# Laying out split operands so that the addresses of a matmul's moving operand and of the next weights keep one difference

## The chip, the core and the metric

The kernel runs on one core of a Trainium2 chip. The core has five engines with their own instruction streams: TensorE (PE in the profile; PEld is its weight load), VectorE (DVE), ScalarE (ACT), GpSimd (POOL) and SyncE (SP), which here only issues DMAs. They share the on-chip memory SBUF (128 partitions; an operand is a stretch of bytes in each partition) and wait for each other through semaphores. TensorE multiplies a stationary operand, the weights (128x128, loaded by a weight load of its own that runs while the previous matmul streams), with a moving operand (128 x up to 512) and adds into PSUM. The metric is device time in microseconds; lower is better.

## What is computed

One layer of a decoder trunk in float32: D = 1024, 512 positions and 16 meta tokens ahead of them. All products below have to be good to float32 accuracy.

```python
h = concatenate([meta, x])                   # (1, 528, 1024)
u = rms_norm(h, norm_gain)
rq, rk, rv, rg, gq, gk, gv, gg, glr, m_ret, m_gla = split(u @ w_in)
o_ret = retention(rope(rq), rope(rk) / 16, rv)         # 4 heads, 256 keys, 512 values
o_ret = head_group_norm(o_ret) * silu(rg)
log_a = log_sigmoid(glr @ w_gate_up + b_gate) / 16
o_gla = gla(gq, gk, gv, log_a)                         # 4 heads, 128 keys, 256 values
o_gla = head_rms_norm(o_gla) * silu(gg)
merged = sigmoid(m_ret) * (o_ret @ w_branch_ret) + sigmoid(m_gla) * (o_gla @ w_branch_gla)
out = rms_norm(h + merged @ w_out)[:, 16:]
```

Nearly all the arithmetic is in the projections `u @ w_in` (11,280 columns), the two branch products and `w_out`.

## The kernel before

**Split operands.** TensorE works on float32 operands in a rounded form (`float32r`). To keep accuracy each operand x is split into `hi`, its rounded form (a copy on ACT), and `lo = x - hi` (a subtraction on DVE): `split`, L154. A product then takes three passes, hi·hi, hi·lo and lo·hi, into one PSUM sum. `mm3` (L189, L192, L193) issues them in that order; `quad` (L318), `proj_a` (L425) and the first projection (L640) write them out.

**`quad`.** Most projections go through `quad`, which forms two 256-column blocks of the result from 7 products instead of 8 (Strassen's scheme in Winograd's form). The activations stand in seven split forms: A11, A12, A22 and the sums S1 to S4. Each product takes one form and one 512x256 block of weights or a sum of blocks (made on DVE), splits that block with `prepare`, and then does 2 column tiles x 4 k x 3 passes = 24 matmuls. With `rows` the activation form is the stationary operand and the weights' block moves (256 columns); otherwise the block's columns are stationary and the form moves (256 columns, or 264 where `wide` takes the meta tokens along). Order of the products: A11, A12, S2, S3, S1, A22, S4; with `early` A11, S3, S2, A12, S1, A22, S4.

**Where operands lie.** Split weights come from `wsplit`: one tile for hi and one for lo, tags `whi` and `wlo`, three buffers each, rows of 256 columns (1024 bytes). The normalized activations lie in `xh`, `xl` (two tiles each, of 4 k x 2 halves x 272 columns; a half is 1088 bytes, a k 2176), which hold A11, A12, A22 and A21; the sums S1 to S4 have tiles `fh3` to `fh6` and `fl3` to `fl6` (4 x 272). A21 is read by `proj_a` alone (`gq0`, `gk0`), not by any product of `quad`. The forms of the GLA branch lie in tiles that the GLA stage has freed (`form_tiles`), with rows of 1024 bytes. Retention heads 0 to 2 are turned into `oh`, `ol` (rows of 2048 bytes), head 3 into the places of `xh0` and `xl0`; the merged activations go to the places of `xh1`, `xl1` and two freed tiles, their sums to those of `fh3` to `fl6`.

**Order of the stages.** First projection and norms; `gla_qk(0)` with the forget gates woven in (`forget_gates`, whose ACT and DVE work is put in a written order by `act` and `vec`); GLA heads 0, 1 with `gla_g(0)`; `gla_qk(1)`, `gla_v(1)`; GLA heads 2, 3 woven into `gla_g(1)`, `gates_first` and `gla_branch` (which uses `quad` with the forms of the GLA output); then for each retention head `ret_qk`, `ret_g`, `ret_v` with the attention of the head before, and for heads 1 and 2 `gates_gla` in turn with `ret_branch` (128x512 matmuls with the turned head moving); `ret_branches` for heads 2 and 3; last the output projection: `wo_first` (256 columns by `mm3`), one `quad` (`wo1`), and the last 256 columns by `mm3`. `weave` alternates a dense generator (matmuls of projections) with a chain of attention steps.

In `forget_gates` the copies of S1 and S3 (`form`) are made ahead; S2 and S4 and the DVE parts of all four follow:

```python
        forms.append(form(S2, u00))
        next_weights(0)
        forms.append(form(S4, u01))
        for i in (2, 0, 1, 3):
            forms[i]()
```

## Time and profile before

| | us |
|---|---|
| median of 3 runs (763.56 to 764.13) | 763.91 |
| span of the profiled execution, first to last instruction | 762.2 |
| DVE busy | 611.2 |
| ACT busy | 451.2 |
| HBM read / written | 104.44 MB / 11.53 MB |

The profile holds one execution; its own time is given as the span, and what a run takes beside the span isn't in it. Times are microseconds from the span's start, means are in ns. A matmul's listed duration is longer than its share of PE, since matmuls overlap: the distance between starts is what counts. Two groups show the splits' price on both engines (columns: line, engine, operation, output<-inputs, shapes, count, then busy us and mean ns, then idle time of the engine ahead of them and who ended it):

```profile
L154 ACT CAST rv_h<-rv_w 128x1024 fp32r<-128x1024 f32 x24 | 25.2, 1052 | 26.9 <-DVE rv_w L371 9.6
L154 DVE TENSOR_TENSOR rv_l<-rv_w,rv_h 128x1024 fp32r<-128x1024 f32 x24 | 29.3, 1221 | 9.2 <-ACT rv_h L154 9.2
```

## The change

It moves operands to other addresses and reorders passes; the number and shapes of matmuls, splits and DMAs stay. In the new constants a lane is a step of `LANE` = 16 elements, 64 bytes, and counts modulo 4.

- `two_forms` puts hi and lo of a pair of forms into one tile, 2 x 2176 elements with 32 elements of gap, in alternating order; `s3` does so for S3 with rows of 288. So hi and lo of a form lie 2 lanes apart, as do neighbouring k.
- S4 has no tile of its own any more: it takes A21's place, and so is formed after `values(1)`, when `gk0` has read A21, and no longer beside S2.
- `wsplit` makes one tile `ws` of 2240 elements (three buffers) for hi and lo, shifted by a number of lanes that the caller gives: interleaved rows of 544 elements (hi at 0, lo at 288), or, with a second number `x`, hi and lo one behind the other at lanes of their own.
- `prepare` asks for the lane of the product's form + 3 with `rows`, + 1 otherwise; for the GLA branch and the output projection tables give the lanes (`G_AT`, `M_AT`).
- `quad` (without tables) and `proj_a` do the three passes of an odd k in the order lo·hi, hi·hi, hi·lo.
- Retention head 3, the merged activations and their sums share tiles that hold hi and lo together.

```diff
+BY_PRODUCT = {1: A11, 2: A12, 3: S4, 4: A22, 5: S1, 6: S2, 7: S3}
+X_AT = 3
+LANES = [X_AT + n for n in (0, 0, 1, 0, 1, 0, 1)]
+O_AT = 2
+M_AT = [(X_AT + 2, X_AT + 2), (1, 2)]
+G_AT = {A11: (1, 1), A12: (2, 2), S4: (2, 2), S1: (2, 2), S2: (2, 2), S3: (0, 2), A22: (0, 0)}
+PASSES = ((0, 0), (0, 1), (1, 0))
...
+    def two_forms(name, swap):
+        t = cp.tile([P, 2 * FW + 2 * LANE], F32R, tag=name, name=name)
+        return [t[:, o:o + FW].rearrange("p (k n c) -> p k n c", k=4, n=2)
+                for o in ((0, FW + 2 * LANE), (FW + 2 * LANE, 0))[swap]]
...
-    def wsplit(shape, name):
-        return (wp.tile(shape, F32R, tag="whi", name=f"{name}_h", bufs=3),
-                wp.tile(shape, F32R, tag="wlo", name=f"{name}_l", bufs=3))
+    def wsplit(shape, name, w=0, x=None):
+        t = wp.tile([P, WT], F32R, tag="ws", name=f"{name}_s", bufs=3)
+        o = LANE * ((w - W_AT) % 4)
+        if x is None:
+            v = t[:, o:o + 4 * 544].rearrange("p (k c) -> p k c", k=4)
+            return v[:, :, :256], v[:, :, 288:]
+        n = int(np.prod(shape[1:]))
+        parts = [t[:, a:a + n] for a in (o, o + n + LANE * ((x - w) % 4))]
+        return [a.rearrange("p (k c) -> p k c", k=shape[1]) if len(shape) > 2 else a for a in parts]
...
         def prepare(i, w):
-            hi, lo = wsplit([P, 4, 256], f"{name}_{i}")
+            form, d = BY_PRODUCT[i], 3 if rows else 1
+            at = (LANES[form] + d,) if lanes is None else [a + d for a in lanes[form]]
+            hi, lo = wsplit([P, 4, 256], f"{name}_{i}", *at)
...
-                    for j, (x1, x2) in enumerate(((0, 0), (0, 1), (1, 0))):
+                    passes = PASSES if lanes is not None or kk % 2 == 0 else PASSES[2:] + PASSES[:2]
+                    for j, (x1, x2) in enumerate(passes):
...
-    def branch(src, row0, oh, ol, name, evac, bank=ppt):
+    def branch(src, row0, oh, ol, name, evac, bank=ppt, at=0):
         for q in range(4):
             raw = wraw(f"{name}_{q}_w")
-            hi, lo = wsplit([P, 4, 256], f"{name}_{q}")
+            hi, lo = wsplit([P, 4, 256], f"{name}_{q}", at, at)
...
-        forms.append(form(S4, u01))
-        for i in (2, 0, 1, 3):
+        for i in (2, 0, 1):
             forms[i]()
...
         values(1)
+        form(S4, u01)()
...
-                    hi, lo = wsplit([P, 4, 256], f"br{h}_{q}")
+                    hi, lo = wsplit([P, 4, 256], f"br{h}_{q}", *((O_AT, O_AT), (X_AT, X_AT))[h - 2])
...
-        w = wsplit([P, 4, 256], f"wo{o}_{kh}")
+        w = wsplit([P, 4, 256], f"wo{o}_{kh}", *[a + 3 for a in M_AT[kh]])
```

## What I predict

> **What bounds the kernel now.** I read the page first (busy time, then the shares of the chain that ended last), then the chain of waits in order of time, then PE's timeline, because the change touches nothing but where matmul operands lie.

> ```profile
> span 762.2 us, 14057 instructions
> ...
> PE 750.4 (98%) x5595; PEld 701.5 (92%) x5595; DVE 611.2 (80%) x873; ACT 451.2 (59%) x764; POOL 133.4 (17%) x172
> ...
> PE 87%; DVE 9%; issue 2%; ACT 1%; POOL 0%; POOLq 0%; DVEq 0%
> ```

> PE is busy for 98% of the span and is 87% of the chain. DVE holds 9%. So the time is PE's number of matmuls times their start-to-start distance (I call it the pitch), and DVE is next behind. A matmul's own duration is no use here, since matmuls overlap; the chain's rows are, because a row is the time in which PE did 24 matmuls in a row (one "block": one product of `quad`, or one 24-matmul group elsewhere).

> ```profile
> 255.01 2.93 PE rqk_b L318 x24
> 257.94 2.92 PE rqk_c L318 x24
> ...
> 275.26 2.85 PE rg_b L318 x24
> ```

> ```profile
> 381.33 2.80 PE mg_c L318 x24
> ```

> A block of 128x256 matmuls takes 2.80 to 2.85 us (I take 2.83, 118 ns each); one with a moving operand 264 wide takes 2.92 (122 ns). Almost every block of the kernel looks like this, whatever the stage. A few don't:

> ```profile
> 232.76 5.70 PE bg_b L318 x48
> 238.46 2.82 PE bg_c L318 x24
> 241.28 2.74 PE bg_b L318 x24
> 244.02 2.72 PE bg_a L318 x24
> 246.74 2.72 PE bg_b L318 x24
> 249.46 2.83 PE bg_c L318 x24
> 252.29 2.73 PE bg_b L318 x24
> ```

> These are the second half of the GLA branch (`gla_branch`, j=1) at the same shape, the same clock and without waits, yet four blocks run at 2.72 to 2.74 (113.5 ns) and others at 2.83. What differs is addresses. Count an SBUF address in lanes: steps of 64 bytes, modulo 256 bytes, so lanes 0 to 3. For each matmul take the lane of the weights that are loaded meanwhile, those of the next matmul, less the lane of its own moving operand: D. In this branch every row of a tile is 1024 bytes and hi and lo are a multiple of 256 apart, so D is constant inside a block. Adding up the sizes of the tiles ahead in the pools gives D=1 for S2, A12, S1 and S4 (241.28, 244.02, 246.74, 252.29: all fast), D=3 for A22 (249.46) and D=2 for A11. The first block of the 5.70 row is S4 of j=0: also D=1, but slow (5.70 is twice 2.85). So D=1 held constant can run in two ways, 113.5 or about 118 ns, and it stays for the block in the one that it entered.

> Another constant stands in the output projection, where D=0:

> ```profile
> 734.74 0.28 PE L318 MATMUL wo_c<-wo_h,msh 128*128 128x256 f32 x1
> 734.86 0.28 PE L318 MATMUL wo_c<-wo_l,msh 128*128 128x256 f32 x1
> 734.98 0.28 PE L318 MATMUL wo_c<-wo_h,msl 128*128 128x256 f32 x1
> 735.10 0.28 PE L318 MATMUL wo_c<-wo_h,msh 128*128 128x256 f32 x1
> 735.22 0.28 PE L318 MATMUL wo_c<-wo_l,msh 128*128 128x256 f32 x1
> 735.34 0.28 PE L318 MATMUL wo_c<-wo_h,msl 128*128 128x256 f32 x1
> ```

> Starts 120 ns apart: D=0 is the slowest constant. Everywhere else D changes every three matmuls, because the activation tiles have rows of 1088 or 2176 bytes (17 or 34 lanes) and the weights rows of 1024 (16): the 118 of the other blocks is a mix.

> The 512-wide matmuls of the retention branches give the opposite preference. Head 2 (D=1) runs until 679.69, head 3 (D=0) after it:

> ```profile
> 676.89 0.39 PE L189 MATMUL br_p<-oh,br_h 128*128 128x512 f32 x1
> ...
> 679.69 0.39 PE L189 MATMUL br_p<-oh,br_h 128*128 128x512 f32 x1
> ...
> 681.07 0.39 PE L189 MATMUL br_p<-oh,br_h 128*128 128x512 f32 x1
> ...
> 683.79 0.39 PE L189 MATMUL br_p<-oh,br_h 128*128 128x512 f32 x1
> ```

> Twelve matmuls take 2.80 us with D=1 (233 ns) and 2.72 us with D=0 (227 ns).

> **The change, part by part.** It removes no matmul, split or transfer. It sets D.

> *256-wide blocks.* In the new layout hi and lo of an activation form lie 2 lanes apart, each row adds 2 lanes, and the weights' tile (`wsplit`) has the same steps: rows of 2176 bytes, lo 1152 bytes (2 lanes modulo 256) behind hi. With passes in the order hi-hi, hi-lo, lo-hi for even k and lo-hi, hi-hi, hi-lo for odd k, I walked through the six steps: each gives the same D, and the lane chosen in `prepare` (activation + 3 where the form is the stationary operand, + 1 where it moves) makes it 1. `G_AT` and `M_AT` do the same for the GLA branch and the output projection. There are 23 quads of 7 products, 161 blocks; 25 of them are 264 wide; with 4 of `gq0` and 8 of `wo_p` that leaves 148 blocks of 256. Six run at 2.72 or so already: three of j=1 besides the last, S4, and S2 and A12 of j=0. So 142 can gain, at most 2.83 - 2.72 = 0.11 us each, 15.6 us. Since D=1 has two rhythms I weigh them by what the trace has: of seven full-clock blocks with D=1, six are fast, but of four entries into such a stretch three ended fast. Between products D is off for one matmul wherever the forms' lanes differ (three times in a quad), so entries count too. I take 0.8 fast: a block of 2.74, gain 0.09, 142 x 0.09 = 12.8 us. Ends: all fast 15.6; none fast (2.83) 0.

> *264-wide blocks* (25, and 4 of `gk0`): no constant D of this width stands in the trace. The eight more columns cost 2.92 - 2.83 = 0.09 us a block now; the bounds are 2.72 + 0.09 = 2.81 and no change at 2.92. I take 0.8 of the way, 0.09 x 29 = 2.6 us (ends 0 and 3.2).

> *512-wide matmuls.* `branch` and `ret_branches` get D=0 for all heads: 96 matmuls each of heads 0, 1 and 2 go from 233 to 227, 288 x 6.6 ns = 1.9 us; head 3 has it already.

> Sum on PE: 12.8 + 2.6 + 1.9 = 17.3 us.

> [...]

> *What the sum loses.* Only 87% of the chain is PE. The rest is DVE, ACT and issue, mostly at the merge before the output projection, where the chain goes through DVE; a faster PE waits there. 17.3 x 0.87 = 15.1. Then there are stages in which DVE is full already (columns: PE, PEld, DVE, ACT, POOL busy):

> ```profile
> 40.00:60.00 20.00, 20.00 (x166) 19.87 (x166) 19.32 (x28) 18.47 (x30) 1.59 (x2) 1.00 0.54 109
> ...
> 280.00:300.00 20.00, 20.00 (x187) 18.94 (x186) 19.93 (x24) 13.25 (x20) 8.27 (x4) 1.00 0.39 107
> ...
> 600.00:620.00 20.00, 19.85 (x182) 18.52 (x181) 19.97 (x27) 13.49 (x24) 2.37 (x5) 1.00 0.40 123
> ```

> At 3% less PE time each would have to fit in some 19.4 us: over by 0.5 and 0.6 in the last two, near zero in the first. With the 19 us stages around 340, 460 and 720 I take 1.6 us. Left: 13.5 us.

> *The S4 form moves* from the middle of `gk0` to after `values(1)`, into the place of x's second half, first K half, which `gk0` has read by then. It issues no DMA, only two instructions:

> ```profile
> L682 ACT CAST fh<-u 128x1056 fp32r<-128x1056 f32 x4 | 4.3, 1073 | 0.0
> ```

> ```profile
> L685 DVE TENSOR_TENSOR fl<-u,fh x4: 1250/1250/1251, 40.1 to 43.6; 128x1056 fp32r<-128x1056 f32 x4
> ```

> ACT gets 1.07 us and DVE 1.25 us later. Behind them on DVE stand the adds and the split for `gg0`'s third product, behind them on ACT a table load and the first decays; if DVE gained nothing from the earlier gap, PE would be late by 1.25 us at that product. But DVE is the full engine of the 40 to 60 stage, so what was taken out ahead comes back: I take 0, ends -1.25 and +1.25. Its reader, the last product of `gg0`, comes some 20 us later.

> *Shared tiles.* hi and lo of split weights are now one tile of three buffers instead of two of three. If the first matmul of a block had to wait for lo as well, it would wait at most one matmul longer (118 ns; two where weights are stationary), as the next pass reads lo anyway. PE now waits for a lo in one place:

> ```profile
> PE bg_b L318 <- DVE bg_l L154: 1.3, 1, 1.3
> ```

> So: 0, end +1 us. The ACT and DVE operations keep their sizes; only row steps differ. After that wait PE also runs a stretch at half clock (granted 0.91 over that stage); whether it returns is worth up to 1.7 us either way:

> ```profile
> 220.00:240.00 20.00, 17.94 (x138) 17.54 (x137) 17.14 (x16) 10.69 (x14) 3.47 (x2) 0.91 0.84 203
> ```

> **Sum and time.** 13.5 us off the profiled span: 762.2 to 748.7. The median of the runs shown, 763.91, is 1.7 us above the span; I take the same there: **750.4 us**.

> **Rivals.**
> 1. *Fast everywhere, and the supply keeps up.* All blocks at 2.72: 15.6 + 3.2 + 1.9 = 20.7, between 18.0 (x 0.87) and 20.7 of it kept: 743.2 to 745.9. For it: once entered, the 113.5 ns rhythm never left by itself in the trace. Against it: S4 of j=0 at 2.85, and DVE's full stages.
> 2. *The 118 ns rhythm of D=1 is common.* A quarter to a half of the blocks fast: 142 x 0.0275 or 0.055, + 0.8 or 1.6, + 1.9 = 6.6 or 11.3; x 0.87 - 1.6 = 4.1 or 8.2: 755.7 to 759.8.
> 3. *Addresses don't matter*, or D is not what I worked out, and the fast blocks of the GLA branch have another cause (their tiles, their stage): 763.9. The heads' 2.80 against 2.72, in one stage, speaks against it. [...]
> 4. *Slower: constant D locks the streams in step in the worst place.* One mechanism, every block from `gv1` to the end: a constant D keeps whatever relation it enters, and the output projection shows one at 120 ns, above the mix. At 2.88 a block, 142 x 0.05 + 6 x 0.16 = 8.1, the 264s at 2.96 another 1.2, less 1.9 for the heads: +7.4 us, 771.3. It decides from a mean block of about 2.84 up. Against it: that is D=0, and no block with D=1 is that slow in the rows.

> **How the numbers follow.** Forecast (746 to 755.5) 0.56, rival 1 0.14, rival 2 (to 762) 0.14, rival 3 0.08, rival 4 0.08. About 0.2% is what a measurement of this kernel can tell from no change. Faster: 0.56 + 0.14 + 0.14 = 0.84; same 0.08; slower 0.08. Range: from rival 1's lower end, 743, to 760, rival 2's upper end; left out are rivals 3, 4 and edges, under 0.2.

> **What would show it.** Chain rows of 24: `rg`, `rv`, `mr`, `mg` at 2.72 to 2.75, `rqk` at 2.81 to 2.83, `wo` starts 113 to 114 ns apart instead of 120; branch matmuls of heads 0 to 2 at 227. DVE's share of the chain above 9%, with new PE waits for `rg_l` or `rv_l` near 290 and 605. I am wrong if blocks stay at 2.83 with D constant (rival 2 or 3), if they show 2.88 (4), or if PE gains but the span doesn't, with PE waiting on DVE (then the 0.87 is too high).

## The result, and the profile after

The changed kernel takes **766.35 us** (median of 6 runs, 766.18 to 766.46); the kernel before, beside it, 763.82 (763.20 to 764.13). The ratio is 1.0033, 95% interval 1.0021 to 1.0045: slower by 0.33%, where 1.8% faster was forecast. The page of the changed kernel, the lines that answer to those shown of before:

```profile
span 764.4 us, 14037 instructions
...
PE 751.2 (98%) x5595; PEld 702.2 (92%) x5595; DVE 611.7 (80%) x873; ACT 451.0 (59%) x764; POOL 133.8 (18%) x172
...
PE 82%; DVE 10%; ACT 4%; issue 3%; POOL 1%; POOLq 0%; DVEq 0%; ACTq 0%
```

The same number of matmuls, as much PE time as before, and less of the chain on PE (82% against 87%): PE got hardly faster, and a few waits were added. The chain in order of time shows both halves of this in the stage of `rqk` and `rg`:

```profile
259.60 2.94 PE rqk_c L347 x24
262.54 2.93 PE rqk_b L347 x24
...
277.00 2.82 PE rg_b L347 x24
279.83 2.82 PE rg_a L347 x24
282.65 2.82 PE rg_b L347 x24
285.47 2.82 PE rg_c L347 x24
```

The blocks that were to take 2.74 take 2.82, where before they took 2.83 and 2.85; the 264-wide ones take 2.93 to 2.94 as before. Yet the change does what it says: with the tiles' addresses put beside the matmuls of the trace, D is 1 at nearly every step inside these blocks. Their starts lie, over and over, 115, 123, 116, 118, 118 and 117 ns apart, 117.8 on average. Blocks near 113.3 are found only in the GLA branch and in the output projection, where the forms' rows are multiples of 256 bytes.

Three figures sum this up: the distances from each matmul's start to the next, summed by width (those above 1.3 times the median are waits and left out).

| us | before | after | mean before | mean after |
|---|---|---|---|---|
| 256 wide | 419.0 (3557 matmuls) | 417.8 (3551) | 117.80 ns | 117.66 ns |
| 264 wide | 84.3 (694) | 84.7 (694) | 121.5 ns | 122.1 ns |
| 512 wide | 154.0 (666) | 151.8 (662) | 231.2 ns | 229.3 ns |

The sums hold different numbers of matmuls, so the means are what to compare: the 256-wide matmuls gained 0.14 ns each, 0.5 us in all, and the 512-wide ones 1.9 ns each, 1.3 us.

And this is where the end moved by 2.2 us in the two profiled executions (start of the same matmul, after less before):

| stretch | us |
|---|---|
| start-up, to the first `gg0` product | +0.46 |
| `gg0`, products S2 and S3 (S4 form moved) | +0.79 |
| turning the GLA output (`got1`) | +0.39 |
| first branch blocks of heads 0 and 1 | +0.31, +0.38 |
| `rg3`, product A22 | +0.98 |
| branches of heads 2 and 3 | -0.54 |
| everything else | -0.55 |

The waits of PE name what is late: for `gg_s` and `rg_s`, splits on DVE, PE did not wait before.

```profile
PE bg_b L347 <- DVE bg_s L173: 1.3, 1, 1.3
...
PE rg_c L347 <- DVE rg_s L173: 0.8, 1, 0.8
...
PE gg_b L347 <- DVE gg_s L173: 0.4, 1, 0.4
```

## The experiments

Eleven kernels were run. Times are medians; each ratio is to the kernel before on the same chip.

**1. Lanes that stand still.** In the fast blocks of before not only D was constant: every row is 1024 bytes and hi and lo are a multiple of 256 apart, so both operands stay on one lane. In the change both hop by 2 lanes at most steps and only their difference stays. e1 lets them stand:

```diff
-FW = 8 * HW
+FW = 4 * 576
-        return [t[:, o:o + FW].rearrange("p (k n c) -> p k n c", k=4, n=2)
-                for o in ((0, FW + 2 * LANE), (FW + 2 * LANE, 0))[swap]]
+        return [t[:, o:o + FW].rearrange("p (k c) -> p k c", k=4)[:, :, :2 * HW]
+                .rearrange("p k (n c) -> p k n c", n=2) for o in (0, FW)]
-            at = (LANES[form] + d,) if lanes is None else [a + d for a in lanes[form]]
+            at = [LANES[form] + d] * 2 if lanes is None else [a + d for a in lanes[form]]
-                    passes = PASSES if lanes is not None or kk % 2 == 0 else PASSES[2:] + PASSES[:2]
+                    passes = PASSES
```

(S3's rows become 320 elements; the output projection's lanes follow.)

> Layout of the changed kernel, but with every row a multiple of 256 bytes and hi and lo in the same lane, so that not only D stays 1 inside a block but also the lane of the moving operand and the lane of the weights; passes in the old order. Theory A (the rhythm needs both lanes to stand still, and a constant D with both lanes jumping by two from matmul to matmul is no better than a mix): a good part of the 256-wide blocks falls from 2.83 to 2.72 us; half of 142 blocks would give -8 us, 758; three quarters 754. Theory B (D is all that counts, and the changed kernel sits in the 118 ns rhythm of D=1): blocks stay at 2.83, 765 to 767.

Measured: 761.71 us, ratio 0.9971 (0.9960 to 0.9982), 4.6 us under the change's median and faster than both kernels. Its chain in the stage shown above:

```profile
269.08 2.92 PE rqk_c L347 x24
272.00 2.74 PE rqk_b L347 x24
274.74 2.83 PE rg_b L347 x24
277.57 2.83 PE rg_a L347 x24
280.40 2.83 PE rg_b L347 x24
283.22 2.74 PE rg_c L347 x24
285.96 2.72 PE rg_b L347 x24
288.69 2.83 PE rg_c L347 x24
```

Now the two rhythms of the prediction appear, in every stage: of the stretches of 10 or more matmuls with D=1, 53 (1500 matmuls) run at 113.3 ns, 56 (1574) at 117.8, and 2 are mixed. So of these layouts D=1 gives the choice of 113.3 only with still lanes, and then about half the blocks take it. The mean distance of the 256-wide matmuls falls to 116.25 ns, 1.4 less than in the change, which is 5.0 us; the 8 us that the expectation put on half of the blocks did not all come.

**2. Constancy of D alone.** e4 is the change with the old order of passes; the lanes hop as before, and D repeats 1, 1, 3 (so every third step is off, not every sixth as the expectation has it):

```diff
-                    passes = PASSES if lanes is not None or kk % 2 == 0 else PASSES[2:] + PASSES[:2]
+                    passes = PASSES
```

> The changed kernel with the old order of passes for odd k, so that D is no longer constant (1, and 3 at every sixth matmul or so) while both lanes jump by two as before. Theory A: it makes no difference, blocks 2.82 to 2.86, 765.5 to 767.5. Theory B: D varies again, so blocks get slower or mixed, above 768 or below 764.

Measured: 766.82 us, ratio 1.0036 (1.0023 to 1.0050), as the change. But not because nothing moved: the mean distance of the 256-wide matmuls rises from 117.66 to 118.18 ns (1.8 us on 3551 of them), and the 264-wide sum falls to 82.1 (-2.6 us on as many matmuls), 20 of these 25 blocks at 116.7 to 117.7 ns. In its chain the 264s are now the shorter ones:

```profile
257.67 2.80 PE rqk_c L347 x24
260.47 2.81 PE rqk_b L347 x24
...
271.77 2.85 PE rqk_b L347 x24
274.61 2.85 PE rg_b L347 x24
```

So in this layout the order of passes with constant D costs the wide blocks no less than it gives the others. The order also sets at which steps the lanes hop, so e4 alone can't say which of the two does it.

**3. Which D?** e2 is e1 with D stepping through the 16 multiples of 16 bytes, one after the other, product by product.

> As e1, but D goes through the 16 multiples of 16 bytes from product to product (7 steps of 16 bytes further each time), both lanes standing still inside a product. A look at block times by D. Theory A: blocks differ by D, from 2.72 (113.5 ns) at some to 2.88 (120 ns) near D=0, each D with one or two rhythms. Theory B: the same blocks differ by at most what stood in the trace of before at 0, 64, 128 and 192 bytes, and nothing lies under 2.72. Total time anything from 755 to 770.

Measured: 765.17 us (one run). Pitch of the full-clock 256-wide blocks by D in bytes, lowest to highest block, worked out from the starts in the trace:

| D | ns | D | ns | D | ns | D | ns |
|---|---|---|---|---|---|---|---|
| 0 | 119.6–120.0 | 64 | 113.3 or 117.8 | 128 | 118.4–120.0 | 192 | 117.8 |
| 16 | 116.8–118.5 | 80 | 118.7–119.4 | 144 | 113.4–119.9 | 208 | 116.7–119.2 |
| 32 | 118.2–118.6 | 96 | 117.1–118.6 | 160 | 119.7–120.0 | 224 | 116.6–116.9 |
| 48 | 118.3–123.7 | 112 | 113.3, else 118.6–120.3 | 176 | 118.1–120.2 | 240 | 116.8–120.1 |

(One of the 13 blocks at 64 bytes holds a mixture, 118.5.) Two blocks of `rv0` in its chain, D=0 and then D=112:

```profile
300.49 2.87 PE rv_a L350 x24
303.36 2.72 PE rv_b L350 x24
```

At the D chosen stands the lowest distance there is with still lanes, but only in some of its blocks (and in one at 112); 224 bytes gave 116.6 to 116.9 in every block, hardly above the mean of the blocks at 64. None of the 264-wide blocks of this run went below 119.9 ns.

**4. The S4 form's move alone**, in the kernel before, with its own tile:

```diff
-        forms.append(form(S4, u01))
-        for i in (2, 0, 1, 3):
+        for i in (2, 0, 1):
...
         values(1)
+        form(S4, u01)()
```

> The kernel before with one part of the change alone: S4 is formed after the last step of the forget gates, in its own tile. If this move makes the wait that the changed kernel shows at the third and fourth product of gg0: +0.7 us from there on, 764.3 to 764.8. If that wait comes from the new tiles of the split weights instead: 763.8, no wait.

Measured: 765.25 us, ratio 1.0017 (1.0008 to 1.0027), 1.3 us more, above the 0.7 expected, with the wait where it was looked for. ACT and DVE in the timeline of e3 (start, duration, operation, and idle time ahead with who ended it):

```profile
60.30 1.06 ACT L682 CAST fh<-u 128x1056 fp32r<-128x1056 f32 x1
61.38 1.28 ACT L816 ACT_TABLE_LOAD   x1
...
63.25 1.05 ACT L154 CAST gg_h<-gg_w 128x1024 fp32r<-128x1024 f32 x1
```

```profile
61.81 1.25 DVE L685 TENSOR_TENSOR fl<-u,fh 128x1056 fp32r<-128x1056 f32 x1
...
64.33 1.23 DVE L154 TENSOR_TENSOR gg_l<-gg_w,gg_h 128x1024 fp32r<-128x1024 f32 x1 [0.59 <-ACT gg_h L154]
```

The same two steps before the change:

```profile
62.10 1.06 ACT L154 CAST gg_h<-gg_w 128x1024 fp32r<-128x1024 f32 x1 [0.23 <-DVE gg_w L371]
```

```profile
63.24 1.22 DVE L154 TENSOR_TENSOR gg_l<-gg_w,gg_h 128x1024 fp32r<-128x1024 f32 x1
```

The cast of S4 stands ahead of the table load on ACT. The weights' cast behind it comes 1.15 us later, DVE waits 0.59 us for that, and the split that PE needs is 1.09 us later; PE itself reaches this product only 0.50 us later, so it waits. From there to the first product of `gqk1` PE falls back by another 0.77 us in e3, and by 0.79 in the change. What was taken out of the earlier gap did not come back. (The 0.50 is there ahead of `gg0`, most of it from the start-up, which comes between 0.4 us earlier and 0.9 us later in the profiles of these kernels, so it can't be put down to an edit.)

**5. S4 in a later gap.** e6 asks for it in the first GLA attention, behind the meta state's transposes, with e1's lanes:

> e1_fixed_lanes with the S4 form copied and split about 10 us later, after the meta state's transposes in the first GLA attention (at 72 to 78 us), where DVE and ACT have idle time, instead of at 62 us ahead of the weight splits of gg0's S2 product; it is first read at about 81 us. Theory A (the move of S4 costs by delaying those splits; e3_s4_late gave +1.3 us for it): the 0.6 us wait before product 6 of gg0 and the shift before product 7 go, 760.2 to 760.8 us against 761.7. Rival B (the wait only moves to product 3, which reads S4, or to gg0's later splits): 761.4 to 762.5 us.

Measured: 761.79 us, ratio 0.9977 (0.9966 to 0.9988), no change against e1. But its DVE step stayed at 62.23 us (62.16 in e1): its later place in the program's text did not move it, and nothing else held it back. So it did not test the place. e9 (below, with e5's lanes) ties it behind the second decay's exponentials:

> e5_kicks with the S4 form tied behind the exponentials of the second decay of the first GLA attention (about 78 us), so that it cannot stand ahead of gg0's weight splits; in e6_s4_slack it still ran at 62.2 us, where it ran in e1 (62.2), so that run did not test its place. Theory A (S4 ahead of the splits costs 1.3 us, as e3 showed): waits of PE on gg_s in gg0 fall by about 1.3 us, 759.2 to 759.8 us against 760.7. Rival B (the product that reads S4 at 85 us waits for it, or its two instructions delay the next splits by as much): 760.4 to 762.

Measured: 765.33 us, ratio 1.0020 (1.0010 to 1.0030), 4.6 us more than e5: its rival, and more than that. The 0.6 us wait for `gg_s` in `gg0` that e5 has is gone, and these are in its place:

```profile
PE go L1018 <- DVE gS L1009: 1.3, 1, 1.3
...
PE gf L948 <- ACT gX L951: 0.8, 1, 0.8
...
PE gs L1007 <- ACT gkmt L1001: 0.3, 1, 0.3
```

S4 then holds up the attention's own steps: up to the fifth product of `gg0` PE is 0.9 us ahead of e5, and between there and the first of `gqk1` it loses 5.3 us. Both later places cost; the early one of the kernel before was the cheap one.

**6. What chooses the rhythm.** In e1, where one block follows another without a wait, the next one's rhythm hung on D at the one step between them: behind D=0 a 117.8 block was followed by one at 113.3 all six times. e5 gives the forms lanes by which that step has D=0 before A11, S2, S1 and S4 and D=1 before the others:

```diff
-LANES = [X_AT + n for n in (0, 0, 1, 0, 1, 0, 1)]
+LANES = [3, 3, 1, 1, 2, 2, 0]
-                .rearrange("p k (n c) -> p k n c", n=2) for o in (0, FW)]
+                .rearrange("p k (n c) -> p k n c", n=2)[:, :, :, :HW] for o in (LANE * at, FW + LANE * at)]
+    x0h, x0l = two_forms("xx0", 272, 0)
+    x1h, x1l = two_forms("xx1", 288, 0)
+    s0h, s0l = two_forms("ff0", 272, 2)
```

> e1_fixed_lanes with other lanes for the activation forms, so that the step from one product to the next has D = 0 before four of the seven products of a quad (A11, S2, S1, S4) and D = 1 before the other three; inside a product both lanes stand still at D = 1 as in e1. In e1 (761.71 us) the blocks ran either at 113.3 ns (1500 matmuls) or at 117.8 ns (1574 matmuls), and the six times that a 117.8 block was followed without a stall by a step with D = 0, the next block ran at 113.3; steps with D = 2 or 3 ended at 117.8 as often as not. Theory A: the rhythm is chosen at the entry, a D = 0 step leads into 113.3 and a D = 1 step keeps what was there. Then at least half of the 1574 slow matmuls turn: 0.5 to 1.0 of 1574 x 4.5 ns = 3.5 to 7.1 us less, 754.6 to 758.2 us, and the count of slow blocks falls from 56 to under 28. Rival B: D = 0 only swaps the two rhythms (or the stalls decide): about as many slow blocks as in e1, 761 to 762.5 us.

Measured: 760.70 us, ratio 0.9961 (0.9947 to 0.9975); 60 stretches fast (1690 matmuls), 57 slow (1423). Its rival was right, though its range began at 761: a step with D=0 swaps the rhythms, from fast to slow as well as back (50 of 51 such steps up to here). The 1.0 us against e1 is about what 190 more fast matmuls give at 4.5 ns (0.85 us). e7 is e5 with e6's edit:

> The lanes of e5_kicks and the place of S4 of e6_s4_slack together. If both theories A hold, their gains add: 753 to 757.2 us. If only the place of S4 counts, 760.2 to 761; if only the D = 0 steps count, 754.6 to 758.2; if neither, as e1_fixed_lanes, 761.7.

Measured: 761.24 us, ratio 0.9966 (0.9953 to 0.9979), between e1 and e5, with 1572 fast and 1565 slow matmuls: the mixture varies from kernel to kernel.

The swap rule was read off those runs, so e8 tests it on an arrangement of its own, D=0 before A11, A12, S3 and S1 (`LANES = [3, 2, 0, 0, 2, 1, 0]`, tiles shifted to match):

> As e5_kicks, but with the four D = 0 steps of a quad placed before A11, A12, S3 and S1, and D = 1 before S2, A22 and S4. A rule read off e1 and e5 afterwards is put to the test on an arrangement it was not read from. Rule: at D = 1 with still lanes a 256-wide block has one of two rhythms, 113.3 or 117.8 ns; a single D = 0 step between two blocks without a stall swaps them (50 of 51 seen), a D = 1 step keeps the one there was. So in each unbroken quad (rg, rv) A11 and S3 must have the other rhythm than A12, S2, S1, A22 and S4, which share one. Rival (the rhythm belongs to the form, its tile or the wait before it): A11, A12, S2 and S3 keep the rhythms of e5 or of e1. The time follows from where the stalls leave the rhythm: 5 of 7 blocks fast gives 757 to 759 us, 2 of 7 gives 762 to 764, an even mixture 760.5 to 761.5.

Measured: 760.48 us, ratio 0.9958 (0.9943 to 0.9973). `rg0` in its chain, A11 to S4:

```profile
274.41 2.83 PE rg_b L349 x24
277.24 2.74 PE rg_a L349 x24
279.98 2.72 PE rg_b L349 x24
282.70 2.83 PE rg_c L349 x24
285.53 2.74 PE rg_b L349 x24
288.26 2.72 PE rg_c L349 x24
290.99 2.72 PE rg_b L349 x24
```

A11 and S3 are slow, the other five fast, as the rule says (2.74 is a 2.72 block with the change of rhythm in it). Over the kernel all 19 single steps with D=0 between two unbroken stretches swapped, 10 up and 9 down, and the steps with D=1 between unbroken blocks of the quads kept the rhythm, as in these rows those before S2, A22 and S4 keep 113.3. `rv0` goes in the other way round, A11 fast and A12 slow. So 1596 matmuls were fast and 1518 slow, an even mixture again. What decides which of the two a block takes after a wait or after other matmuls is still open. e10 adds e9's place of S4:

> The lanes of e8_adjacent with the place of S4 of e9_kicks_s4. If the place of S4 is worth 1.3 us, this is 1 to 1.5 us below e8_adjacent; if the rival of e9 holds, within 0.5 us of it. The same swap rule must hold block by block as in e8.

Measured: 764.86 us, ratio 1.0016 (1.0007 to 1.0026), 4.4 us above e8 and outside both expectations: the late S4 costs as much here, lost in the same stretch. The rhythms swap as in e8.

**7. The wide blocks.** e11 is e8 with D repeating 1, 3, 1 in the 264-wide products, from the weights' lanes alone:

```diff
+            if wide and i not in (3, 5):
+                at[1] += 2
             hi, lo = wsplit([P, 4, 256], f"{name}_{i}", *at)
```

> e8_adjacent with one more edit: the 264-wide products of the wide quads (gqk, rqk) get the lo part of their weights 2 lanes behind hi. The moving operand still stands on one lane, but D is no longer constant there: it repeats 1, 3, 1 from matmul to matmul. In e4_plain_passes the 264-wide blocks ran at 116.7 ns with the repeating D of 1, 1, 3 and both operands hopping by 2 lanes, against 120 to 121.7 ns in every kernel with D = 1 constant (e1, e5, e8: 120.0 to 121.7; after: 121.6 to 122.2). Theory A (the repeating pattern of D is what this width wants, whichever operand hops): the 25 blocks of gqk and rqk at 116.7, 24 x 3.9 ns = 0.09 us less each, 2.3 us in all, 758.0 to 758.8 us against 760.5. Rival B (the moving operand has to hop too, or the pattern of e4 had another cause): blocks at 120 to 122, 760 to 761.5 us.

Measured: 760.81 us, ratio 0.9959 (0.9946 to 0.9971); the blocks run at 120.2 to 120.8 ns, one at 121.6. The rival holds: a repeating D does not do it while the moving operand stands still. e4's 116.7 needs something else of its layout; that both operands hop there is the difference left, and it wasn't tried apart.

## Why the prediction was wrong

**The failing step** is in "256-wide blocks": "each gives the same D", and from it two rhythms with 0.8 of the blocks fast, 12.8 us. The first half came true, D is 1; the conclusion doesn't follow from it. The rows it rested on (241.28, 244.02, 246.74, 252.29) had constant D and still lanes at once, which the prediction said ("every row of a tile is 1024 bytes and hi and lo are a multiple of 256 apart") and then used for D alone. With hopping lanes D=1 gives about 117.8 ns (the change), with still lanes 113.3 or 117.8 (e1), with still lanes and other D mostly 117 to 120 (e2). The term measured 0.5 us in the change. With so little gained on PE, the factor 0.87 and the 1.6 us for full DVE stages were not put to the test.

**The share of fast blocks**, 0.8 from a handful of rows, was mis-sized as well: with the lanes put right it is about half (e1, e5, e8: 49%, 54%, 51% of the matmuls that are in one of the two rhythms). A swap at each step with D=0 (19 of 19 in e8) keeps it there; the prediction took such entries for harmless.

**264 wide**: 2.6 us forecast, -0.4 measured. No row of this width with constant D stood in the trace, and 0.8 of the way was a guess; D=1 constant gave 120.0 to 121.7 ns with still lanes (e1, e5, e8) and 121.6 to 122.2 with hopping ones (the change), and the pattern with 116.7 to 117.7 in 20 of 25 blocks (e4) isn't constant.

**512 wide**: right in its direction, too large in size: 1.9 us forecast, about 1.2 measured. The branches of heads 2 and 3, where only head 2 changes, gave back 0.54 of 96 x 6.6 ns = 0.63. Heads 0 and 1 gave some 0.3 each: of their four blocks of 24 the later three start 231.2, 230.6 and 228.6 ns apart on average where 233 stood before, and 227 comes only at the end. In e1, with the same lanes in this stage by the sizes of the tiles, the same three blocks of both heads take 227.5, 227.0 and 226.6. So D=0 doesn't fix the rhythm at this width at once either; why it came late in the change is open.

**S4's move**: priced 0 with an end of +1.25. The end was near the truth: e3's median is 1.3 us longer, and its trace shows 0.77 of that behind the move. The prediction named the queue rightly (adds and splits on DVE, the table load on ACT) and was wrong that the gap ahead would give it back.

**Shared tiles**: the end of +1 us was not reached in the way that was named. The first matmul of A22 in `rg3` doesn't wait for lo; the second, which reads it, does, because lo comes later: in the change four steps on `ol` stand ahead of this split on DVE, before it was three. The timeline of PE and of DVE in the change, then DVE before, where the fourth step on `ol` comes ahead of the split of the next product only:

```profile
608.08 0.28 PE L347 MATMUL rg_c<-rg_s,xx 128*128 128x256 f32 x1
609.12 3.00 PE L347 MATMUL rg_c<-rg_s,xx 128*128 128x256 f32 x23 [0.76 <-DVE rg_s L173]
```

```profile
606.46 0.87 DVE L522 SCALAR_TENSOR_TENSOR ol<-ot,rgain,oh 128x256 fp32r<-128x256 f32 x2
607.25 0.68 DVE L1250 TENSOR_TENSOR rpq<-rpq,rpq 128x512 f32<-128x512 f32 x1
607.85 2.35 DVE L173 TENSOR_TENSOR rg_s<-rg_w,rg_s 128x1024 fp32r<-128x1024 f32 x2
```

```profile
604.77 1.22 DVE L154 TENSOR_TENSOR rg_l<-rg_w,rg_h 128x1024 fp32r<-128x1024 f32 x1
605.91 0.47 DVE L492 SCALAR_TENSOR_TENSOR ol<-ot,rgain,oh 128x256 fp32r<-128x256 f32 x1
606.31 1.21 DVE L154 TENSOR_TENSOR rg_l<-rg_w,rg_h 128x1024 fp32r<-128x1024 f32 x1
```

In the change the window from 600 to 620 shows DVE busy for 20.00 of 20 us (19.97 before), so the wait is DVE's queue, in another order; e3, which has the old tiles, doesn't show it. Which of the tile edits reordered DVE wasn't taken apart.

**The rivals.** Rival 2 (118 common) is what happened to the lanes once they stood still; rival 3's time, 763.9, was nearest, though not its reason: e2's 113.3 to 123.7 ns on one layout shows that addresses matter. Rival 4's mechanism, all blocks locked at 120, is what D=0 does in e2 (119.6 to 120.0), and D=1 in none of its 13 blocks there (113.3 or 117.8, one at 118.5). What made the change slower was none of the four: the waits around S4 and `rg3`, 0.79 + 0.98 us of the 2.2, with too little gained on PE to cover them. The smaller losses at `got1` and at the first branch blocks, 0.39 and 0.69 us, were not traced to a cause.

## What to carry to other kernels

When a few fast rows are explained by one property, list what else those rows share, and build the smallest variant that has the one without the other before laying a whole layout on it. A rhythm that can lock in two ways is worth its mean, not its best (in e1 116.25 ns, not 113.3). And an instruction moved "into a gap" has to be followed on both of its engines to the split that PE reads next: here 1.06 us on ACT ahead of a table load put PE back by 0.77 us.
